# First half of the MLP as seven block products, with the high weight part streaming against both activation parts

## The chip, the cores and the metric

The kernel runs on one core of one Trainium2 chip. Its time is device microseconds (us) of one execution; of the kernel before, three runs gave a median of 2058.57 us (2057.65 to 2058.89). One more execution was taken with the hardware profiler, and all views below are of that one.

## The reference: what is computed

One encoder block on 512 tokens of width 2048, all in float32. `P`, `D` and `DFF` in the kernel are 128, 2048 and 8192. The change lies in the last three lines and in what leads over to them.

```python
h = rmsnorm(x, norm_mix_pre)
proj = h @ w_in                                  # 2048 x 5120
mix = concat(pool_mixer(...), hgrn2_mixer(...)) @ w_out
x = x + rmsnorm(mix, norm_mix_post)
h = rmsnorm(x, norm_mlp_pre)
ff = square(relu(h @ w_mlp_in)) @ w_mlp_out      # 2048 x 8192, then 8192 x 2048
x = x + rmsnorm(ff, norm_mlp_post)
```

## The kernel before

Every large matrix product keeps float32 accuracy with single-pass `float32r` products: each operand is split into a high part (a rounding copy on ACT) and a low part (the difference, on DVE), and a product of two blocks becomes three: high x high, high x low, low x high. The product of the low parts is left out. A weight block is 512 x 512 elements, 1024 KB; it is loaded raw, split in two halves (`w_split_gen` L200, later `split_gen` L875: 128x1024 elements per instruction), and used.

The stages, in order of time:

- **Input projection** (`pj`), the two mixers beside it, and the **output projection** (`om`, four groups of `gemm_group`, L258). The results of `om` are normed, added to the residual stream and kept in `Y` (`residual_task`, L768).
- **First half of the MLP** (`mi`, L947 to L960): 16 groups of 512 columns of `w_mlp_in`. The activations `h2` (transposed by `feed_h` on TensorE at L384, then split by ACT and DVE at L385 and L386) stay in SBUF as four pairs. In a group, each of four weight blocks is stationary in 128x128 pieces, and all 512 tokens stream against each piece: `block` (L241) issues `wh,ah`, `wh,al`, `wl,ah`. That is 16 groups x 4 blocks x 4 column pieces x 4 row pieces x 3 = 3072 products with 512 moving columns. Four PSUM banks collect a group; `evac_in` (L834) does relu and the row scale on DVE (L837), the square on ACT (L838), and writes the result to DRAM (`h1_dram`, L839).
- **Second half of the MLP** (L979 to L1072): for each of 8 pieces of 1024 rows of `w_mlp_out`, a 2 x 2 block scheme with seven products instead of eight (`ORDER`, L851). A slot is one of the seven products on one half `q` of the columns: 112 slots of 24 products (`products`, L979) with 512 moving columns. Here the activations are stationary and the weights stream. Sums of weight blocks are made by DMAs that add into SBUF (L889, from POOL's queue); sums of activation blocks by DVE (L910), which are then split (L906, L907). `act_steps` (L912) lists these steps, and `pend` (L1039) says from which slot each may be issued.
- **The end**: `finish_rows` (L1017) norms the result, adds the residual stream read back from DRAM, and writes the output: rows of the first 256 tokens at slot `base + 9`, the rest after the last slot.

Each engine works off its own queue in the order in which the program lists the instructions. In a slot, the split of the next slot's weights comes first on ACT and DVE, then what else is due. ACT can overwrite the high part `mHI` of slot k + 1 only once slot k - 1 has ended, since there are two `mHI` and two `mLO` tiles.

Of the kernel before, what the change touches and what calls it, by code (L numbers as in the profile page):

```python
# [28 lines left out]
def hybrid_block(  # L29
# [34 lines left out]
    psg_pool = tc.tile_pool(name="psg", bufs=4, space=PSUM)  # L64
    psg = psg_pool.__enter__()
# [4 lines left out]
    h1_dram = dram.tile([DFF, T], F32, name="h1_dram")  # L70
# [154 lines left out]
    def new_pair(nm):  # L225
        h = pairs.tile([P, 4, 512], F32R, tag="ph", name=nm + "h")
        l = pairs.tile([P, 4, 512], F32R, tag="pl", name=nm + "l")
        return h, l
# [26 lines left out]
    def new_banks(name):  # L255
        return [psg.tile([P, 512], F32, tag="g", name=f"{name}_{j}") for j in range(4)]

    def gemm_group(name, acts, w_stationary, evac, feeder=None, merge=0):  # L258
# [47 lines left out]
        if merge:  # L306
            ws = []
            for _ in range(merge):
                if wnext["split"] <= unit_no[0]:
                    w_split(4)  # L310
                    w_dma()
                ws.append(take_unit())
            if banks is None:
                banks = new_banks(name)
            for j in range(4):
                for k in range(merge):
                    ui = n - merge + k
# [3 lines left out]
                    clock.tick()  # L321

# [11 lines left out]

    for c in range(NC):
        for u in range(4):
            wlist.append((w1, u * 512, c * 512))
# [400 lines left out]
    def late_pools():  # L738
        clock.drain()
        hg.__exit__(None, None, None)  # L740
        yp = ctx.enter_context(tc.tile_pool(name="yp", bufs=1))
        tp2 = ctx.enter_context(tc.tile_pool(name="tp2", bufs=2))
        late["tp2"] = tp2
        late["Yall"] = yp.tile([P, NT, D], F32, name="Y")
        late["Y"] = [late["Yall"][:, t, :] for t in range(NT)]
# [18 lines left out]
    h2 = []  # L764
# [3 lines left out]
    def residual_task(t):  # L768

        Y = late["Y"]  # L770
        if t == 0:
            h2.extend(new_pair(f"h2{u}") for u in range(4))
        rt = row_rstd(t)
        for u in range(4):
# [4 lines left out]
            if t == 3:  # L779
                yield 1  # L780
        nc.gpsimd.dma_start(x2_dram[t * P:(t + 1) * P, :], Y[t])
        if t < 3:
            yield 3
            row_square(t)

    def feed_h(u, kt):
        Y = late["Y"]
        c = u * 512 + kt * P
        feed(h2[u], kt, [Y[t][:, c:c + P] for t in range(NT)], vcol("mpre", u * 4 + kt))

# [6 lines left out]
    def norm2_task():  # L797
        row_square(3)
        yield 1
# [4 lines left out]
        yield from row_bcast(rbc, rstd2)  # L804

    def load_xr(t):
        xr = pairs.tile([P, D], F32, tag="ph" if t < 2 else "pl", name=f"xr{t}")
        nc.gpsimd.dma_start(xr, x2d[t * P:(t + 1) * P, :])
        late["xr", t] = xr
# [13 lines left out]
    for n in range(4):  # L823
        if n == 2:
            for t in range(NT):
                load_xr(t)
        gemm_group(f"om{n}", MixActs(), False, evac_mix(n), merge=2 if n == 3 else 0)
    clock.add(norm2_task(), 4)
    keep_warm(12)


    tp2, Yall = late["tp2"], late["Yall"]

    def evac_in(c):  # L834
        def f(j, bank):
            r = tp2.tile([P, 512], F32, tag="tmp", bufs=2, name="r")
            nc.vector.scalar_tensor_tensor(out=r, in0=bank, scalar=0.0, in1=rbc, op0=ALU.max, op1=ALU.mult)  # L837
            nc.scalar.activation(out=r, in_=r, func=AF.Square)  # L838
            nc.gpsimd.dma_start(h1_dram[c * 512 + j * P:c * 512 + (j + 1) * P, :], r)  # L839
        return f  # L840
# [9 lines left out]
    NP = NC // 2  # L850
    ORDER = (1, 2, 5, 3, 6, 7, 4)  # L851
    slots = [(p, i, q) for p in range(NP) for i in ORDER for q in range(2)]
    st = {"X": {}, "YZ": {}, "HI": {}, "LO": {}, "A": {}, "r": {}, "S": {}}

    def w2_block(p, a, b, q):
        r0, c0 = (2 * p + a - 1) * 512, (2 * q + b - 1) * 512
        return w2[r0:r0 + 512, c0:c0 + 512].rearrange("(kt p) c -> p kt c", p=P)

    def load_x(x):

        if x < 2 * NP:
            nc.sync.dma_start(st["X"][x % 3], w2_block(x // 2, 1, 1, x % 2))

    def load_yz(n):

        if n < 4 * NP:
            p, k = divmod(n, 4)
            nc.sync.dma_start(st["YZ"][n % 3], w2_block(p, 2, 1 + k // 2, k % 2))

    def raw_of(p, i, q):  # L870
        if i in (1, 5, 6, 4):
            return st["X"][(2 * p + q) % 3]
        return st["YZ"][(4 * p + q + (0 if i == 2 else 2)) % 3]

    def split_gen(k):  # L875
        if k >= len(slots):
            return
        p, i, q = slots[k]
        raw, hi, lo = raw_of(p, i, q), st["HI"][k % 2], st["LO"][k % 2]
# [8 lines left out]
        if more:  # L888
            nc.gpsimd.dma_start(raw, w2_block(p, *more, q), accum_op=ALU.add)  # L889
        elif i == 4:  # L890
            load_x(2 * p + q + 3)
        else:
            load_yz(4 * p + q + (0 if i == 2 else 2) + 3)

    def load_r(p):
        if p < NP:
            for h in range(2):
                c = 2 * p + h
                nc.sync.dma_start(st["r"][h], h1_dram[c * 512:(c + 1) * 512, :].rearrange("(j p) t -> p j t", p=P))

    def r_block(tp, kh):
        return st["r"][kh - 1][:, :, (tp - 1) * 256:tp * 256]

    def split_a(i, src):
        a = st["A"][i]
# [3 lines left out]
    def sum_s(dst, a, b, op):  # L909
        nc.vector.tensor_tensor(out=st["S"][dst], in0=a, in1=b, op=op)  # L910

    def act_steps(p):  # L912

        S = st["S"]
        return [
            (1, lambda: split_a(1, r_block(1, 1))),
            (2, lambda: split_a(2, r_block(1, 2))),
            (0, lambda: sum_s(0, r_block(2, 1), r_block(2, 2), ALU.subtract)),
            (5, lambda: split_a(5, S[0])),
            (0, lambda: sum_s(1, S[0], r_block(1, 1), ALU.subtract)),  # L920
            (0, lambda: sum_s(0, r_block(1, 2), S[1], ALU.add)),
            (3, lambda: split_a(3, S[0])),
            (6, lambda: split_a(6, S[1])),
            (0, lambda: sum_s(1, r_block(1, 1), r_block(2, 1), ALU.subtract)),
            (7, lambda: split_a(7, S[1])),
            (4, lambda: (split_a(4, r_block(2, 2)), load_r(p + 1))),
        ]

    def new_act(i, tag):
        st["A"][i] = pairs.tile([P, 2, 4, 256], F32R, tag=tag, name=f"a{i}")  # L930

    def y_block(tp, n):
        return Yall[:, 2 * tp - 2:2 * tp, n * 512:(n + 1) * 512]

    def begin_split():
        for k in ("HI", "LO"):
            st[k][0] = wspl.tile([P, 4, 512], F32R, tag=k.lower(), name=f"m{k}0")
        return split_gen(0)

    def begin_x(x):  # L940
        st["X"][x] = wraw.tile([P, 4, 512], F32, tag="raw", name=f"X{x}")
        load_x(x)

    behind["dma"] = [lambda: begin_x(0), lambda: begin_x(1)]
    behind["split"] = [begin_split]

    for c in range(NC):  # L947
        gemm_group(f"mi{c}", h2, True, evac_in(c), feeder=feed_h if c == 0 else None)
        if c == NC - 4:
            for h in range(2):  # L950
# [144 lines left out]
```

## Time and profile before

| | |
|---|---|
| median of three runs | 2058.57 us |
| the profiled execution, its own time | 2058.64 us |
| its span (first to last instruction) | 2056.9 us |
| PE (matrix products) busy | 2028.0 us, 99% of the span |
| PEld (loads of the stationary operand) busy | 1680.0 us, 82% |
| DVE busy | 1065.0 us, 52% |
| ACT busy | 698.8 us, 34% |
| first product of `mi` to first product of the second half | 713.97 to 1418.42 us |
| last product | starts at 2042.6 us |

How to read it: PE is TensorE with its products, PEld the loads of its stationary operand, DVE is VectorE, ACT ScalarE, POOL GpSimd, SP the engine that issues most DMAs. The ends of products are modelled: the record of a 128x512 product lasts 0.39 us, but the next one starts long before. The pace of TensorE is therefore read from starts of successive products, not from busy time. A group's row gives busy us, mean ns of one instruction, and the idle time before it with what ended it. In the timeline the columns are start, duration, engine, line, operation, out<-in, shapes and count.

### The profile page before, as it was taken

The numbers are of one execution on the slowest core, as the hardware profiler recorded it, in microseconds if no ns is written. First come the engines' busy times: TensorE is split into PE (matmuls) and PEld (weight loads), VectorE is DVE, ScalarE is ACT, GpSimd is POOL, SyncE is SP. The second block draws the span as 40 slices with busy tenths as digits, with TensorE's granted clock in tenths as the row PEclk, the third lists the DMA queues.
The fourth block names the chain that finished last, engine by engine and source line by source line (L and its number), as shares of the span: only waits on it lengthen the run. The fifth ranks groups of instructions, "written<-read, shape, count | busy, mean of one in ns | idle before, by whom it ended". The sixth has DMA issues, their size and how long they took to land. (4 is left out here: it accounts for less than half of the span.)

```text
span 2056.9 us, 22509 instructions
## 1 busy us (share of the span) xinstructions
PE 2028.0 (99%) x9354; PEld 1680.0 (82%) x9354; DVE 1065.0 (52%) x1170; ACT 698.8 (34%) x865; POOL 130.7 (6%) x197
## 2 busy tenths in 40 slices
PE   9999999999999999999999999999999999999995
PEld 7888888888888888888888888887888888888884
DVE  4547443754623452222322222334778778778877
ACT  5322232223222342222222222223554444444443
POOL 1000000000000000000000000000110110110110
PEclk9999999999999999999999999999999999999998
DMA  5322222222353343433343333546998998998994
GB/s 189 109 82 82 83 80 84 83 66 80 108 188 103 123 143 123 123 119 106 118 146 114 114 123 108 178 145 186 239 222 210 227 224 217 224 221 225 218 214 134
DMA packets 144933, 302.43 MB, mean 147 GB/s; under 512 B 5752, under 2 KB 8896, under 8 KB 143040
## 3 DMA queue, kind: packets, MB, share of 16 engines
q1 hardware_dynamic: 104432, 207.64, 30.9%
q0 software_dynamic: 40400, 93.36, 21.4%
q8 instruction: 73, 1.20, 0.2%
q14 instruction: 28, 0.23, 0.0%
HBM read 275.81 MB, written 25.17 MB: 146 GB/s over the span
## 5 line engine op out<-in xcount | busy, mean ns | idle before, releaser
L216 DVE TENSOR_TENSOR wl<-wr,wh 128x1024 fp32r<-128x1024 f32 (+1 forms) x246 | 289.3, 1197 | 431.7 <-ACT wh L215 431.5
L215 ACT CAST wh<-wr 128x1024 fp32r<-128x1024 f32 (+1 forms) x246 | 244.9, 1024 | 387.4 <-PE mi L252 241.6
L987 PE MATMUL al<-mHI,a 128*128 128x512 f32 x1024 | 318.9, 391 | 1.5 <-ACT mHI L882 1.5
L987 PE MATMUL ga<-mHI,a 128*128 128x512 f32 x768 | 238.9, 391 | 1.6 <-ACT mHI L882 1.6
L987 PEld LDWEIGHTS al<-mHI,a 128*128 128x128 f32 x1024 | 193.5, 189 | 42.3 <-ACT mHI L882 1.9
L987 PE MATMUL al<-mLO,a 128*128 128x512 f32 x512 | 200.5, 392 | 5.4 <-DVE mLO L883 5.4
L882 ACT CAST mHI<-X 128x1024 fp32r<-128x1024 f32 x128 | 133.8, 1053 | 145.5 <-PE ga L987 69.9
L987 PEld LDWEIGHTS ga<-mHI,a 128*128 128x128 f32 x768 | 145.0, 189 | 32.2 <-ACT mHI L882 2.0
L883 DVE TENSOR_TENSOR mLO<-X,mHI 128x1024 fp32r<-128x1024 f32 x128 | 150.8, 1219 | 13.6 <-ACT mHI L882 13.6
L987 PE MATMUL ga<-mLO,a 128*128 128x512 f32 x384 | 150.4, 392 | 0.8 <-DVE mLO L883 0.8
L882 ACT CAST mHI<-YZ 128x1024 fp32r<-128x1024 f32 x96 | 100.5, 1054 | 118.4 <-PE al L987 64.4
L837 DVE SCALAR_TENSOR_TENSOR r<-mi,rbc 128x512 f32<-128x512 f32 x64 | 44.0, 688 | 165.6 <-PE mi L252 165.6
L838 ACT ACTIVATE r<-r 128x512 f32<-128x512 f32 x64 | 40.5, 632 | 261.9 <-DVE r L837 230.8
L987 PEld LDWEIGHTS al<-mLO,a 128*128 128x128 f32 x512 | 96.8, 189 | 25.9 <-DVE mLO L883 5.7
L883 DVE TENSOR_TENSOR mLO<-YZ,mHI 128x1024 fp32r<-128x1024 f32 x96 | 113.0, 1219 | 4.3 <-ACT mHI L882 4.3
L252 PE MATMUL mi<-h20h,wh 128*128 128x512 f32 x256 | 100.0, 391 | 0.8 <-ACT wh L215 0.8
L252 PE MATMUL mi<-h21h,wh 128*128 128x512 f32 x256 | 100.3, 392 | 0.0
L252 PE MATMUL mi<-h22h,wh 128*128 128x512 f32 x256 | 100.0, 391 | 0.0
L252 PE MATMUL mi<-h20h,wl 128*128 128x512 f32 x256 | 99.8, 390 | 0.1
L252 PE MATMUL mi<-h23h,wh 128*128 128x512 f32 x256 | 99.7, 389 | 0.0
L252 PE MATMUL mi<-h20l,wh 128*128 128x512 f32 x256 | 99.7, 389 | 0.0
L252 PE MATMUL mi<-h22h,wl 128*128 128x512 f32 x256 | 99.7, 389 | 0.0
(292 smaller groups left out, 3785.8 us busy)
## 6 DMA issues: line engine op xcount, KB each, us to landing
wr<-in_w_mlp_in SPq DMA_DIRECT2D x64, 1024.0 KB, 5.7
X<-in_w_mlp_out POOLq DMA_DIRECT2D x48, 1024.0 KB, 10.1
wr<-in_w_in SPq DMA_DIRECT2D x39, 1024.0 KB, 5.1
YZ<-in_w_mlp_out SPq DMA_DIRECT2D x32, 1024.0 KB, 6.4
wr<-in_w_out SPq DMA_DIRECT2D x16, 1024.0 KB, 5.1
h_dram<-r POOLq DMA_DIRECT2D x64, 256.0 KB, 3.6
r<-h_dram SPq DMA_DIRECT2D x16, 1024.0 KB, 10.1
X<-in_w_mlp_out SPq DMA_DIRECT2D x16, 1024.0 KB, 5.1
```

The lines of the kernel that those rows point to most:

```text
L215: nc.scalar.copy(out=hi[:, ks, :], in_=raw[:, ks, :])
L216: nc.vector.tensor_tensor(out=lo[:, ks, :], in0=raw[:, ks, :], in1=hi[:, ks, :].bitcast(F32), op=ALU.subtract)
L252: nc.tensor.matmul(bank, l, r, start=first and kt == 0 and oi == 0, stop=last and kt == 3 and oi == 2)
L837: nc.vector.scalar_tensor_tensor(out=r, in0=bank, scalar=0.0, in1=rbc, op0=ALU.max, op1=ALU.mult)
L838: nc.scalar.activation(out=r, in_=r, func=AF.Square)
L882: nc.scalar.copy(out=hi[:, ks, :], in_=raw[:, ks, :])
L883: nc.vector.tensor_tensor(out=lo[:, ks, :], in0=raw[:, ks, :], in1=hi[:, ks, :].bitcast(F32), op=ALU.subtract)
L987: nc.tensor.matmul(bank[:, h, :], a[:, l, kt, ts], r[:, kt, :], start=i in (1, 2, 5) and kt == 0 and oi == 0, stop=kt == 3 and oi == 2, sk ...
```

## The change

The first half of the MLP is written as 112 slots too, with the same seven products as the second half; one list of 224 slots covers both. The tokens are split in two halves of 256, the 2048 input rows in two halves of 1024, and a pair of 512-column weight blocks forms a piece `g` (8 pieces). A slot is one product on 512 of the 1024 input rows (`q`), and stationary is the weight, as before. The moving operand now has 256 columns. Two forms are used:

- In piece 0, three products of 256 columns per 128x128 piece: high x high, high x low, low x high (L1019).
- In pieces 1 to 7, the high weight part meets both activation parts in one product of 512 moving columns (256 of the high part, 256 of the low), whose two results lie side by side in one PSUM bank (L1014); the low weight part then meets the high activation part with 256 columns, added to the first of the two (L1015). The two halves of the bank are added when the bank is emptied (`evac_in`).

The diff, cut to the parts that are spoken of:

```diff
-    for c in range(NC):
-        gemm_group(f"mi{c}", h2, True, evac_in(c), feeder=feed_h if c == 0 else None)
-        ...
+    slots = [(g, i, q) for g in range(2 * NP) for i in ORDER for q in range(2)]
+    def w_block(g, a, b, q):
+        if g < NP:
+            w, r0, c0 = w1, (2 * (a - 1) + q) * 512, (2 * g + b - 1) * 512
+        else:
+            w, r0, c0 = w2, (2 * (g - NP) + a - 1) * 512, (2 * q + b - 1) * 512
...
+    plan = {
+        0: ([feed_step(1, 1, "act"), spl(1, 1, 1, 1)], [feed_step(1, 2, "dve")]),
+        1: ([lambda: new_act(2), spl(2, 0, 1, 2)], [feed_step(1, 3, "act")]),
...
+    def products_in(k, hook):
+        g, i, q = slots[k]
+        main = PA if i in (1, 6, 7, 4) else PG
...
+            if g:
+                o = main[m // 2][:, m % 2].rearrange("p (a b) -> p a b", a=2)
+                nc.tensor.matmul(o, hi[:, kt, ms], r, start=st, stop=False, skip_group_check=True)
+                nc.tensor.matmul(o[:, 0], lo[:, kt, ms], r[:, 0], start=False, stop=sp, skip_group_check=True)
+            else:
+                o = main[0][:, m // 2, (m % 2) * 256:(m % 2) * 256 + 256]
+                for oi, (l, x) in enumerate(((hi, 0), (hi, 1), (lo, 0))):
+                    nc.tensor.matmul(o, l[:, kt, ms], r[:, x], start=st and oi == 0 and m % 2 == 0,
+                                     stop=sp and oi == 2, skip_group_check=True)
+            if n % 4 == 3:
+                hook(n // 4)
...
+    for k in range(n_in):
+        def hook(n):
+            if n == 0:
+                while ends and "rbc2" in late:
+                    ends.pop(0)()
+            if n == 1:
+                for f in amid:
+                    f()
+                evac_in(k, 0)
+        w_split_all(k + 1)
+        for f in before:
+            f()
+        products_in(k, hook)
+        evac_in(k, 1)
+        run_pend(k, 1)
...
-    keep_warm(12)
...
-        if k == base + 9:
-            finish_rows(1)
-    finish_rows(2)
+        if d == 9:
+            for t in range(2):
+                steps.extend(finish_steps(t))
+        for _ in range(2):
+            if steps and d < 13:
+                steps.pop(0)()
```

What goes with it. The activations of the first half are no longer split token row by token row: their transposes (`feed_in`, the same 64 in number) go to raw tiles in SBUF, DVE forms their block sums there (`to_sum`, L893), and each of the seven operands is split (`split_in`, L889 and L890, or L885 and L886 with a minus sign). `plan` spreads these steps over slots 0 to 10. `evac_in` takes results out per half slot: copies on ACT (L1052), additions and subtractions on DVE (L1049, L1067), and `finish_in` does relu, scale and square per 128x1024. Weight sums of the first half come by adding DMAs from POOL's queue too. The second half keeps its products and their order; it has two tiles for the second kind of raw weight block where it had three, its first activation steps (`run_pend`) are issued during the last slots of the first half, the last slot runs its two PSUM banks one after the other, and the finishing steps are spread over slots instead of standing in one block. The 12 calls that kept TensorE busy between `om` and `mi` (`keep_warm`) are gone.

Two places in the order of the instructions. First, PE in the middle of the first half: `mi` is a PSUM bank, `h20h` and `h20l` the high and low activations, `wh` and `wl` the parts of a weight block. Before:

```order
L252 MATMUL mi_1_5361<-h20h,wh_5304 128x512
L252 MATMUL mi_1_5361<-h20l,wh_5304 128x512
L252 MATMUL mi_1_5361<-h20h,wl_5305 128x512
L252 MATMUL mi_1_5361<-h20h,wh_5304 128x512
L252 MATMUL mi_1_5361<-h20l,wh_5304 128x512
L252 MATMUL mi_1_5361<-h20h,wl_5305 128x512
```

The same place in the change; `mo` is a PSUM bank, `a` the activations with both parts, `mh` and `ml` the parts of a weight block:

```order
L1014 MATMUL mo_5629<-a_5098,mh_4643 128x512
L1015 MATMUL mo_5629<-a_5098,ml_4644 128x256
L1014 MATMUL mo_5629<-a_5098,mh_4643 128x512
L1015 MATMUL mo_5629<-a_5098,ml_4644 128x256
L1014 MATMUL mo_5630<-a_5098,mh_4643 128x512
L1015 MATMUL mo_5630<-a_5098,ml_4644 128x256
```

Where three products of 512 columns served 512 tokens, a product of 512 and one of 256 serve 256 tokens.

Second, DVE at the start of the first half. Before, between the residual of the last token rows (L777) and the steady groups, DVE splits weights (`wl`) and transposed activations (`h20l`, `h21l`):

```order
L386 SCALAR_TENSOR_TENSOR h20l<-fps,vec,h20h 128x512
L216 TENSOR_TENSOR wl_4724<-wr_4473,wh_4723 128x512
L777 SCALAR_TENSOR_TENSOR Y<-Y,rt,xr_4141 128x512
L386 SCALAR_TENSOR_TENSOR h20l<-fps,vec,h20h 128x512
L216 TENSOR_TENSOR wl_4724<-wr_4473,wh_4723 128x512
L777 SCALAR_TENSOR_TENSOR Y<-Y,rt,xr_4141 128x512
L386 SCALAR_TENSOR_TENSOR h21l<-fps,vec,h21h 128x512
L386 SCALAR_TENSOR_TENSOR h20l<-fps,vec,h20h 128x512
L216 TENSOR_TENSOR wl_4724<-wr_4473,wh_4723 128x512
```

In the change, in slots 4 and 5: `RU`, `YX` and `A` are raw activations and their sums, `a` the split operands, `ml` the low parts of the weights of slots 5 and 6:

```order
L858 TENSOR_TENSOR ml_4683<-X_4470,mh_4682 128x1024 x2
L893 TENSOR_TENSOR RU<-RU,A_4971 128x1024
L890 TENSOR_TENSOR a_4931<-RU,a_4931 128x1024
L890 TENSOR_TENSOR a_5029<-A_4886,a_5029 128x1024
L893 TENSOR_TENSOR A_4886<-A_4886,YX 128x1024
L893 TENSOR_TENSOR RU<-RU,A_4886 128x1024
L858 TENSOR_TENSOR ml_4644<-YZ_4680,mh_4643 128x1024 x2
L886 SCALAR_TENSOR_TENSOR a_5095<-A_4886,a_5095 128x1024
L890 TENSOR_TENSOR a_5098<-RU,a_5098 128x1024
```

The splits of weights now stand between sums and splits of activations of twice the size, and the operand of slot 5 (`a_4931`) comes after the sum that it is split from.

More of the change, by code (lines that the diff above doesn't have):

```diff
@@ L804, in norm2_task, with load_xr @@
         yield from row_bcast(rbc, rstd2)
[L806 to L809, printed above, removed]
+        late["rbc2"] = True
+    def load_xr(i):
+        xr = pairs.tile([P, 2, D], F32, tag="pp", name=f"xr{i}")
+        for k in range(2):
+            t = 2 * i + k
+            nc.gpsimd.dma_start(xr[:, k], x2d[t * P:(t + 1) * P, :])
+            late["xr", t] = xr[:, k]
     def evac_mix(n):
@@ new lines, in hybrid_block @@
+    behind["dma"] = [lambda: begin_x(0), lambda: begin_x(1)]
+    for n in range(4):
+        if n == 2:
+            load_xr(0)
+            load_xr(1)
+        last = n == 3
+        gemm_group(f"om{n}", MixActs(), False, evac_mix(n), merge=2 if last else 0,
+                   during=during_mix if last else None)
+    tp2, yp = late["tp2"], late["yp"]
+    YZ[0] = tp2.tile([P, 4, 512], F32, tag="big", bufs=1, name="YZ0")
+    load_yz(0)
+    HI[1] = wspl.tile([P, 4, 512], F32R, tag="hi", name="mh1")
@@ L929, in new_act @@
[L929 to L944, printed above, removed]
@@ new lines, in hybrid_block, with run_pend @@
+    pend = []
+    for p in range(NP):
+        for n, (i, free, f) in enumerate(act_steps(p)):
+            pend.append((p, i, f, n_in + 14 * p + max(free - 14, -8 + n)))
+    ready = set()
+    def run_pend(k, most=2):
+        for _ in range(most):
+            if pend and pend[0][3] <= k:
+                p, i, f, _at = pend.pop(0)
+                f()
+                if i:
+                    ready.add((p, i))
+    for k in range(n_in):
+        g = slots[k][0]
+        before, amid = plan.get(k, ([], []))
+        def hook(n):
[8 more added lines that the diff above has]
+        for f in before:
+            f()
+        products_in(k, hook)
+        evac_in(k, 1)
+        run_pend(k, 1)
+        clock.tick()
+        if k >= last_in:
+            begin_out(k - last_in)
+        if k == 13:
+            assert "rbc2" in late
+            pss_pool.__exit__(None, None, None)
+            psm = ctx.enter_context(tc.tile_pool(name="psm", bufs=1, space=PSUM, reuse_waits="tile"))
+            ps_mo = [psm.tile([P, 2, 512], F32, name=f"mo{q}") for q in range(2)]
+            PA, PG = ps_in[::-1], ps_mo
@@ L1001, in evac_out @@
             nc.scalar.copy(out=yv, in_=bank)
-        else:
-            nc.vector.tensor_tensor(out=yv, in0=yv, in1=bank, op=ALU.add if sign > 0 else ALU.subtract)
-        if p == NP - 1 and i in LAST:
-            n = 2 * q + b - 1
-            for t in (2 * tp - 2, 2 * tp - 1):
+            return
+        final = g == 2 * NP - 1 and i in LAST
+        end = k == len(slots) - 1
+        parts = [slice(h, h + 1) for h in range(2)] if end else [slice(0, 2)]
+        for hs in parts:
+            nc.vector.tensor_tensor(out=yv[:, hs], in0=yv[:, hs], in1=bank[:, hs],
+                                    op=ALU.add if sign > 0 else ALU.subtract)
+            if not final:
+                continue
+            for h in range(hs.start, hs.stop):
+                t = 2 * tp - 2 + h
```

464 lines of the change are left out of this document (291 added, 173 removed).

## The prediction

> **What bounds the kernel now.** I read the page's first part, then the table of stretches (us from the span's start: busy time of PE, PEld, DVE, ACT and POOL with their records, granted clock, DMA share, GB/s).
>
> ```profile
> PE 2028.0 (99%) x9354; PEld 1680.0 (82%) x9354; DVE 1065.0 (52%) x1170; ACT 698.8 (34%) x865; POOL 130.7 (6%) x197
> 760.00:1400.00 640.00, 640.00 (x2825) 530.14 (x2824) 183.31 (x181) 154.98 (x180) 31.83 (x59) 1.00 0.41 127
> 1420.00:2040.00 620.00, 610.65 (x2670) 503.79 (x2669) 489.81 (x433) 300.62 (x313) 80.76 (x64) 0.99 0.91 216
> ```
>
> TensorE bounds both halves of the MLP. In the first half everything else is idle most of the time (DVE 183 of 640 us, DMA 41%); in the second, with seven block products, DVE has 490 of 620 us and the DMA engines 91%, and TensorE still lost only some 9 us. So the first half is worth what its products cost, and the price of one is read from their starts. First and last of a run in the timeline of PE, 25 products apart, and one merged piece of the chain that ended last:
>
> ```profile
> 1000.00 0.39 PE L252 MATMUL mi<-h21h,wl 128*128 128x512 f32 x1
> ...
> 1005.67 0.39 PE L252 MATMUL mi<-h22h,wh 128*128 128x512 f32 x1
> 1466.66 43.52 PE al L987 x192
> ```
>
> 5.67 / 25 and 43.52 / 192 both give 0.2267 us for a product of 512 columns with its load. The first half's 3072 products are 696.4 us. Where the stage begins:
>
> ```profile
> 708.57 0.40 PE L252 MATMUL om<-wh,mp1l 128*128 128x512 f32 x1
> 708.80 2.84 PE L365 MATMUL warm_ps<-ones,ident 128*128 128x128 f32 x24
> 711.48 0.49 PE L384 MATMUL fps<-ident,Y 128*128 128x128 f32 x3
> 712.36 0.77 PE L384 MATMUL fps<-ident,Y 128*128 128x128 f32 x5 [0.39 <-DVE Y L777]
> 713.97 0.50 PE L252 MATMUL mi<-h20h,wh 128*128 128x512 f32 x1 [0.85 <-ACT wh L215]
> ...
> 1418.42 0.39 PE L987 MATMUL al<-mHI,a 128*128 128x512 f32 x1
> ```
>
> From 708.80 to 1418.42 are 709.6 us: 696.4 of products, 24 fillers in 2.68 us (0.112 each), 64 transposes at that pace 7.1, and 3.4 of waits and slow restarts.
>
> **The products.** The change has 8 pieces x 14 slots x 16 = 1792 pairs of a 128x128 weight piece and a row piece. In pieces 1 to 7 (1568 of them) each costs one product of 512 columns and one of 256; in piece 0 (224) three of 256. What 256 columns cost no row shows, so I bound it. Below stand, in the timeline, sixteen small products with a full 128x128 load each, the group of loads, and products at half clock with their stretch:
>
> ```profile
> 192.36 1.89 PE L603 MATMUL lps<-Q,K 128*128 128x64 f32 x16
> 194.06 0.48 PE L252 MATMUL pj<-wh,xT2h 128*128 128x512 f32 x1
> L987 PEld LDWEIGHTS al<-mHI,a 128*128 128x128 f32 x1024 | 193.5, 189 | 42.3 <-ACT mHI L882 1.9
> 1430.00:1435.00 5.00, 3.16 (x7) 2.33 (x8) 4.34 (x5) 4.78 (x6) 0.00 (x0) 0.74 0.71 131
> 1432.92 1.05 PE L987 MATMUL ga<-mHI,a 128*128 128x512 f32 x2
> 1433.78 0.63 PE L987 MATMUL ga<-mLO,a 128*128 128x512 f32 x1
> 1434.20 1.05 PE L987 MATMUL ga<-mHI,a 128*128 128x512 f32 x2
> 1435.06 0.63 PE L987 MATMUL ga<-mLO,a 128*128 128x512 f32 x1
> ```
>
> Small products with their loads start every 1.70 / 16 = 0.106 us, so a load can follow a load that fast, and the 189 ns of its record is latency. The fillers with 128 columns stand at 0.112. The floor for 256 columns is therefore 0.112. At half clock five products take 2.14 us, 0.428 each, so the array streams 512 columns in 0.214 at full clock, and 0.013 of the 0.2267 is something else. Is it a fixed part per product, 256 columns cost 0.107 + 0.013 = 0.120; does it scale, 0.113. I take 0.117: load and stream are nearly equal here, and neither can hide all of the other.
>
> The Trainium skill ("TensorE: Matmul & The Clock Gate", "Back-to-back issue gap") gives columns / 2.4 + 2.5 ns for a product by itself, 109 ns for 256 columns as an estimate, which would make the sum 18 us lower; for 512 columns it says 216 where this trace has 227, so I keep to the rows.
>
> Sum: 1568 x (0.2267 + 0.117) = 538.9, 224 x 3 x 0.117 = 78.6, together 617.5 us: **78.9 less** than 696.4. The 64 transposes stay; the 24 fillers go (**2.7 less**).
>
> **What must hide behind a slot.** A slot of pieces 1 to 7 lasts 16 x 0.3437 = 5.50 us. The durations:
>
> ```profile
> L882 ACT CAST mHI<-X 128x1024 fp32r<-128x1024 f32 x128 | 133.8, 1053 | 145.5 <-PE ga L987 69.9 <-PE al L987 66.9 <-ACT a L906 4.5
> L883 DVE TENSOR_TENSOR mLO<-X,mHI 128x1024 fp32r<-128x1024 f32 x128 | 150.8, 1219 | 13.6 <-ACT mHI L882 13.6
> L837 DVE SCALAR_TENSOR_TENSOR r<-mi,rbc 128x512 f32<-128x512 f32 x64 | 44.0, 688 | 165.6 <-PE mi L252 165.6
> L794 ACT ACTIVATE junk<-Y 128x512 f32<-128x512 f32 x16 | 9.8, 620 | 0.0
> 1976.38 2.36 DVE L883 TENSOR_TENSOR mLO<-X,mHI 128x1024 fp32r<-128x1024 f32 x2
> 1978.65 1.22 DVE L1003 TENSOR_TENSOR Y<-Y,ga 128x1024 f32<-128x1024 f32 x1
> ```
>
> Back to back, DVE starts a 128x1024 every (1978.65 - 1976.38) / 2 = 1.14 us. A piece needs of DVE 28 such halves of weight splits (31.9), 20 additions of 128x512 out of PSUM at 0.69 (13.8) and four final steps (4.6): 50 of 77 us. The tightest slot follows product 6: three additions (2.1), then two splits (2.3), which ACT's copies precede by 1.1: done some 5 us into 5.5. TensorE needs the second half only 0.7 us after its slot starts, so I cost this at nothing, with a slip of 1 us in each of 28 such places (28 us) as the price if the cover fails. Two products in a row on one bank (2 and 5, 6 and 7) leave half a slot, 2.7 us, to empty it; the additions need 1.4 to 2.1.
>
> DMA: 14 blocks of 1024 KB and 2 MB of results per piece, the same per slot as the second half, which ran so without a wait:
>
> ```profile
> 1590.00:1670.00 80.00, 80.00 (x354) 66.25 (x353) 64.41 (x56) 37.42 (x37) 10.20 (x8) 1.00 0.92 222
> X<-in_w_mlp_out POOLq DMA_DIRECT2D x48, 1024.0 KB, 10.1
> ```
>
> An adding DMA lands in 10.1 us and is needed four slots, 22 us, after it is issued. On POOL's queue the writes of `x2_dram` and `h1_dram` now stand among the adding DMAs; each waits for a DVE or ACT step no more than a slot away.
>
> **The start of the first half.** Here the cover is gone. Until slot 7 can begin, DVE must pass 34 instructions of 128x1024 (38.8), 16 of 128x512 (11.4) and 12 small ones (2.0): 52.2 us. It can begin 2.6 us after the last `om` product, because ACT's copy of the first weights stands behind four squares of 0.62 with a read of 0.19 each. Following both queues row by row I find some 8 us in which DVE waits for ACT. Slot 7 thus starts 62.5 us after `om`; TensorE's own work until then is 7 slots x 5.6 and 56 transposes, 45.6. That is 17 us of waits, in four pieces of 3 to 4 us (before slots 1, 5, 6, 7), plus 2.5 for a restart at half clock (above: after a wait at 1430 some 12 products at 0.428). **19 more**, bounded by 9 (no wait on ACT) and 28 (twice the waits); the 3.4 of before go.
>
> **Boundary and end.** The pieces of the chain around the second half:
>
> ```profile
> 1432.34 34.32 PE ga L987 x143
> ...
> 2017.56 0.16 DVE Y L1028
> 2017.71 1.04 issue
> 2018.75 3.93 DVE Y L1028 x5
> 2022.68 1.15 DVE mLO L883
> 2023.87 19.16 PE al L987 x71
> 2043.05 1.23 DVE Y L1003
> ...
> 2049.47 3.18 DVE Y L1028 x4
> ```
>
> From 1418.42 to 1466.66 the 192 products of eight slots need 43.5 us and took 48.2: 4.7 lost, as `h1_dram` had first to be read back and summed. In the change these steps are issued eight slots ahead: **4.2 less**. From 1466.66 to 2043.05 the other 2496 products need 565.9 and took 576.4: 10.5 lost, mainly to the finishing block at 2017. Spread over slots 9 to 12 it still puts about 7 us on a DVE that has 5.45, so I see three waits of 2 to 3.5 us: **1 less**. After the last product, 2043.05 to 2056.9, half of the last evacuation moves ahead of it: **1.5 less**.
>
> **Sum.** 2056.9 - 78.9 - 2.7 + 19 - 3.4 - 4.2 - 1 - 1.5 = 1984.2 of span; 1.7 lies outside it (2058.64 - 2056.9), and the profiled run equals the median within 0.1: **1986 us**.
>
> **Rivals.** *A, better:* 256 columns at the floor 0.112 (2240 x 0.005 = 11 less) and a start near its bound (10 to 13 less): 1962. For it speak the fillers at 0.112; against it the 0.013 that every long product shows. *B, slots slip:* evacuations and splits on DVE in one queue overrun, 1 us at 28 places: 2014. For it: 5 of 5.5 us in the tightest slot; against it: the second half ran at 64.4 of 80 us of DVE without a wait. *C, slower than before:* the load of the next weight piece does not hide behind a product of 256 columns, so that each costs load plus stream, 0.106 + 0.107 = 0.213. Then 2240 x (0.213 - 0.117) = 215 more: 2201. The point from which it decides is 0.149 per short product, where the 72 us of gain are used up. Against it: the fillers, whose loads and streams together take 0.112. The Trainium skill (same page, Part 3, "The mechanism") says that a load overlaps running products only when its row group differs, which would be this rival; the trace speaks against that, as 128-row loads do hide behind 512 columns at 0.2267. *That the change does not do what it says* is settled by the order: 512 and 256 alternate in pieces 1 to 7, and piece 0 alone has three short products.
>
> **Chances.** Forecast 0.68, A 0.12, B 0.13, C 0.07. The range holds A's 1962; above, 0.120 per product (7), the start's upper bound (9) and part of B (10) give 2012. A measurement here can tell 0.2%, 4 us. Faster: forecast, A and nearly all of B, 0.91; same 0.02; slower, C, 0.07.
>
> **What would show it.** Right: starts of successive `mo` products alternating 0.227 and about 0.117; slots of 5.5 us; waits on DVE (`a`, `ml`) in the first 62 us after `om`, none after slot 8; no wait at the boundary. Wrong: a pair of products above 0.36 us, waits of TensorE on DVE in every piece, or a DMA share at 1 with TensorE waiting for raw blocks.

## The result and the profile after

The changed kernel takes 2063.18 us (median of nine runs, 2059.75 to 2064.83) against 2057.96 us of the kernel before (nine runs beside it): ratio 1.0022, with an interval of 1.0011 to 1.0032. The forecast was 1986 us. The profiled execution took 2061.68 us, with a span of 2060.0. So 75.8 us of span had to be found between the forecast of 1984.2 and what came.

First the page's first part of the kernel after:

```profile
PE 1975.7 (96%) x10066; PEld 1665.3 (81%) x10066; DVE 1286.0 (62%) x1392; ACT 832.7 (40%) x1009; POOL 195.6 (9%) x229
```

TensorE is busy 52 us less than before, but 96% of the span where it was 99%. The work did shrink; waits have taken its place. Next the bounds of the stages, in the timeline of PE (start, duration, engine, line, operation):

```profile
743.79 0.39 PE L250 MATMUL om<-wh,mp 128*128 128x512 f32 x1
744.03 1.03 PE L913 MATMUL fps<-ident,Y 128*128 128x128 f32 x8
...
860.85 0.40 PE L1014 MATMUL mi<-a,mh 128*128 128x512 f32 x1
...
1000.08 0.40 PE L1014 MATMUL mi<-a,mh 128*128 128x512 f32 x1
1000.32 0.28 PE L1015 MATMUL mi<-a,ml 128*128 128x256 f32 x1
...
1005.63 0.40 PE L1014 MATMUL mi<-a,mh 128*128 128x512 f32 x1
...
1085.26 0.40 PE L1014 MATMUL mi<-a,mh 128*128 128x512 f32 x1
...
1087.38 0.40 PE L1014 MATMUL mi<-a,mh 128*128 128x512 f32 x1
...
1424.66 0.39 PE L1208 MATMUL mo<-mh,o 128*128 128x512 f32 x1
...
2045.05 0.39 PE L1208 MATMUL mo<-mh,o 128*128 128x512 f32 x1
```

The last product of `om` starts at 743.79; before, at 708.57. So 35.2 us were lost **ahead of** the first half, in stages whose products the change does not touch. The first half then takes 680.6 us (744.03 to 1424.66) where 709.6 stood before: 29 us won, not the 66 of the forecast. Sixteen pairs from 1000.08 to 1005.63 give 0.347 us a pair, six from 1085.26 to 1087.38 give 0.353; the forecast had 0.3437.

The list of waits of PE (line, who releases, us in total, times, longest) names the places. In the kernel before, the same list has no row of `om`, and of `pj` only two, at the start of the program:

```profile
PE mi L1014 <- DVE t L1049: 11.9, 7, 6.3
PE om L250 <- DVE Y L811: 11.7, 6, 4.0
PE mi L1019 <- ACT t L1052: 10.3, 6, 4.5
PE mi L1019 <- DVE t L1049: 7.1, 4, 4.6
...
PE pj L250 <- DVE pu L436: 3.8, 4, 1.5
PE pj L250 <- DVE F L515: 3.1, 4, 0.8
PE pj L250 <- ACT G L546: 3.1, 4, 0.8
PE pj L250 <- DVE Q L534: 2.2, 4, 0.8
PE om L250 <- DVE sst L753: 2.2, 2, 1.5
```

Everything that releases TensorE in these rows of `om`, of `pj` and of piece 0 (L1019) is an instruction that empties a PSUM bank, but for `sst` (L753), which DVE runs right behind such an emptying. One such place in the timeline of all engines:

```profile
691.97 0.39 PE L250 MATMUL om<-wh,mp 128*128 128x512 f32 x1
692.45 0.60 ACT L810 ACTIVATE junk<-om 128x512 f32<-128x512 f32 x1 [1.16 <-PE om L250]
...
693.17 0.69 DVE L811 TENSOR_TENSOR Y<-om,wpost 128x512 f32<-128x512 f32 x1 [0.61 <-ACT junk L810]
693.92 0.50 PE L250 MATMUL om<-wh,mp 128*128 128x512 f32 x1 [1.56 <-DVE Y L811]
...
694.26 0.40 PE L250 MATMUL om<-wl,mp 128*128 128x512 f32 x1
```

Bank after bank of a group is finished and emptied. TensorE, done with one bank at about 692.2, stands still until 693.92, when DVE has read that bank, though its next product writes another one. The wait costs more than its 1.56: from 691.97 to 694.26 two products take 2.29 us where two take 0.45 without a wait, 1.84 more. If each wait costs 0.28 more than its row has it, the 24 waits in the rows of `pj` and `om` (26.1 us) make up some 33 of the 35.2, an estimate. Two edits of the diff that the prediction did not speak of give the suspicion:

```diff
-    psg_pool = tc.tile_pool(name="psg", bufs=4, space=PSUM)
...
+    psg = ctx.enter_context(tc.tile_pool(name="psg", bufs=2, space=PSUM))
...
     def new_banks(name):
-        return [psg.tile([P, 512], F32, tag="g", name=f"{name}_{j}") for j in range(4)]
+        g = [psg.tile([P, 2, 512], F32, tag="g", name=f"{name}_{j}") for j in range(2)]
+        return [g[j // 2][:, j % 2] for j in range(4)]
```

The same four banks are held as two tiles of two banks. The suspicion is that a product that writes one bank of a tile then waits until the other bank of the same tile has been emptied.

### The profile page after: what moved, and what is told of

It is laid out like the page before. It is cut to its first block, busy times and chain, and to the rows that moved or that the text cites. A ratio compares the mean times of both kernels' runs of the same rounds, so it can differ in the third digit from the quotient of the medians.

```text
span 2060.0 us, 24502 instructions
## 1 busy us (share of the span) xinstructions
PE 1975.7 (96%) x10066; PEld 1665.3 (81%) x10066; DVE 1286.0 (62%) x1392; ACT 832.7 (40%) x1009; POOL 195.6 (9%) x229
## 4 chain that ended last, share of the span: by engine, by line
PE 88%; DVE 5%; ACT 2%; issue 1%; DMA 0%; DVEq 0%; ACTq 0%; POOLq 0%
PE pj L250 20%; PE mo L1208 16%; PE mi L1208 13%; PE mi L1014 9%; PE om L250 8%; PE mo L1014 8%; PE mi L1015 5%; PE mo L1015 4%; PE mi L1019 3%; PE lps L600 2%; DVE ml L858 1%; DVE t L1049 1%; ACT mh L857 0%; DVE YT L1258 0%; PE po L663 0%
## 5 line engine op out<-in xcount | busy, mean ns | idle before, releaser
L1014 PE MATMUL mi<-a,mh 128*128 128x512 f32 x896 | 316.5, 398 | 11.9 <-DVE t L1049 11.9
L1208 PE MATMUL mo<-mh,o 128*128 128x512 f32 x1024 | 318.5, 391 | 1.1 <-ACT mh L857 1.1
L250 PE MATMUL pj<-xT,wh 128*128 128x512 f32 x768 | 243.3, 397 | 10.9 <-DVE pu L436 3.8
L858 DVE TENSOR_TENSOR ml<-X,mh 128x1024 fp32r<-128x1024 f32 x176 | 207.4, 1220 | 70.3 <-ACT mh L857 70.3
L1015 PE MATMUL mi<-a,ml 128*128 128x256 f32 x896 | 251.1, 280 | 0.0
L1208 PE MATMUL mi<-mh,o 128*128 128x512 f32 x768 | 237.7, 389 | 0.0
L858 DVE TENSOR_TENSOR ml<-YX,mh 128x1024 fp32r<-128x1024 f32 x176 | 207.4, 1220 | 46.1 <-ACT mh L857 46.1
L1014 PE MATMUL mo<-a,mh 128*128 128x512 f32 x672 | 235.2, 395 | 0.0
L1208 PEld LDWEIGHTS mo<-mh,o 128*128 128x128 f32 x1024 | 192.9, 188 | 42.2 <-ACT mh L857 2.2
L1014 PEld LDWEIGHTS mi<-a,mh 128*128 128x128 f32 x896 | 169.3, 189 | 53.7 <-ACT mh L857 7.3
L1208 PE MATMUL mo<-ml,o 128*128 128x512 f32 x512 | 200.3, 391 | 6.4 <-DVE ml L858 6.4
L1015 PE MATMUL mo<-a,ml 128*128 128x256 f32 x672 | 187.5, 279 | 0.0
L1015 PEld LDWEIGHTS mi<-a,ml 128*128 128x128 f32 x896 | 170.0, 190 | 0.0
L1014 PEld LDWEIGHTS mo<-a,mh 128*128 128x128 f32 x672 | 126.1, 188 | 30.0
```

The lines of the kernel that those rows point to most:

```text
L250: nc.tensor.matmul(bank, l, r, start=first and kt == 0 and oi == 0, stop=last and kt == 3 and oi == 2)
L858: nc.vector.tensor_tensor(out=lo[:, ks, :], in0=raw[:, ks, :], in1=hi[:, ks, :].bitcast(F32), op=ALU.subtract)
L1014: nc.tensor.matmul(o, hi[:, kt, ms], r, start=st, stop=False, skip_group_check=True)
L1015: nc.tensor.matmul(o[:, 0], lo[:, kt, ms], r[:, 0], start=False, stop=sp, skip_group_check=True)
L1208: nc.tensor.matmul(bank[:, h, :], a[:, l, kt, ts], r[:, kt, :], start=i in (1, 2, 5) and kt == 0 and oi == 0, stop=kt == 3 and oi == 2, sk ...
```

## Experiments

Times are medians; each kernel ran beside the kernel before on the same chip (2057.2 to 2057.4 us), and the ratio's interval is given. Differences between kernels of different rounds are uncertain by about 1 us, since the medians of the kernel before differ by 0.8 (2057.2 to 2058.0). No kernel below leaves out any part of the computation.

### The tiles of two banks, put into the kernel before

```diff
-    psg_pool = tc.tile_pool(name="psg", bufs=4, space=PSUM)
+    psg_pool = tc.tile_pool(name="psg", bufs=2, space=PSUM)
...
-        return [psg.tile([P, 512], F32, tag="g", name=f"{name}_{j}") for j in range(4)]
+        g = [psg.tile([P, 2, 512], F32, tag="g", name=f"{name}_{j}") for j in range(2)]
+        return [g[j // 2][:, j % 2] for j in range(4)]
```

> The kernel before, with one edit: its four one-bank PSUM tiles of a group become two tiles of two banks, as in the change. Nothing else of the change. Theory A (a product that writes one bank of a tile waits until the other bank of the same tile has been emptied): the projections lose what the change lost there, the first mi product comes some 35 us later than 714, and the 16 groups of the first half lose 1.66 us each as the 10 groups of the input projection did in the change, 27 in all; time about 2119. Theory B (the loss comes from the operand pairs, whose high and low parts now lie in one SBUF tile, so that DVE's writes of the low part hold up TensorE's reads of the high part): no loss here, about 2058.

Measured: 2137.78 us, ratio 1.0389 [1.0368, 1.0410]. Its list of waits:

```profile
PE mi L252 <- DVE r L838: 37.0, 32, 1.5
PE om L252 <- DVE Y L819: 11.4, 6, 3.7
...
PE pj L252 <- DVE pu L440: 3.8, 4, 1.5
PE pj L252 <- DVE F L519: 3.1, 4, 0.8
PE pj L252 <- ACT G L550: 3.1, 4, 0.8
PE om L252 <- DVE sst L757: 3.1, 2, 1.6
PE pj L252 <- DVE Q L538: 2.2, 4, 0.8
```

With nothing else changed, the rows of `pj` and `om` come out as in the kernel after, to the tenth for `pj`, and the old first half gets two such waits in each of its 16 groups. The cause of those waits is the tile, not the block products. Their price was under-estimated, 2119 against 2137.8: the last `om` product starts 36.8 us later, as expected, but the first half lost 47.0 us where 27 were expected, its 32 waits being 37.0 of them.

### One-bank tiles in the changed kernel

```diff
-        g = [psg.tile([P, 2, 512], F32, tag="g", name=f"{name}_{j}") for j in range(2)]
-        return [g[j // 2][:, j % 2] for j in range(4)]
+        return [psg.tile([P, 512], F32, tag="g", name=f"{name}_{j}") for j in range(4)]
...
-    ps_in = [psg.tile([P, 2, 512], F32, tag="g", name=f"mi{k}") for k in range(2)]
-    PA, PG = ps_in[0:1], ps_in[1:2]
+    ps_in = [psg.tile([P, 512], F32, tag="g", name=f"mi{k}") for k in range(4)]
+    PA, PG = ps_in[0:2], ps_in[2:4]
```

(From slot 14 on it takes new tiles of two banks, as in pieces 1 to 7 one emptying instruction reads 256 columns of each of two neighbouring banks.)

> The change, with one-bank PSUM tiles again in the projections and in piece 0 of the first half; the two-bank tiles are opened after slot 13. Operand pairs stay in one tile. Theory A: the projections are back to their time before (last om product near 709 instead of 744), and piece 0 loses its false waits, some 10 to 13 of its 117 us, so that about 104 to 107 stay; together 45 to 48 less, about 2016. Theory B: the last om product stays near 744, time 2050 to 2063.

Measured: 2010.68 us, ratio 0.9774 [0.9759, 0.9789]. Its list of waits no longer has a row of `om` on an emptying step, and what is left in the first half is this:

```profile
PE mj L1014 <- DVE t L1049: 11.6, 7, 6.4
...
PE mi L1019 <- DVE a L890: 2.9, 3, 1.8
PE mi L1019 <- ACT t L1052: 1.8, 1, 1.8
PE mi L1019 <- DVE t L1049: 1.8, 1, 1.8
```

52.5 us came back, a little more than the 45 to 48 expected. The new names in the code (`mj` is the tile from slot 14 on) change nothing in the products.

### One-bank tiles in the projections alone

The edit above for `new_banks`; piece 0 keeps its two tiles of two banks, from a pool of its own:

```diff
+    psg_pool.__exit__(None, None, None)
+    psi_pool = tc.tile_pool(name="psi", bufs=1, space=PSUM, reuse_waits="tile")
+    psi = psi_pool.__enter__()
+    ps_in = [psi.tile([P, 2, 512], F32, name=f"mi{k}") for k in range(2)]
     PA, PG = ps_in[0:1], ps_in[1:2]
```

> The changed kernel with one-bank accumulator tiles in the projections alone; piece 0 of the first half keeps its two tiles of two banks. Theory A (the false waits in the projections and those in piece 0 are separate costs): the projections' last product returns to about 709 us from the span's start, 35 us less, piece 0 stays at 117 us against 100 with one-bank tiles: about 2063 - 35 = 2028 us, and the further 17 us to 2011 belong to piece 0. Theory B (piece 0 is slow because the projections end late or in a bad state, not by its own tiles): piece 0 falls to 100 us by itself and the time to about 2011 us.

Measured: 2031.12 us, ratio 0.9871 [0.9857, 0.9884]. The instructions on the tiles `om`, `mi` and `mj` (count, duration, first to last start), and the rows of its waits that stay:

```profile
L251 PE MATMUL om<-wh,mp x256: 388/389/394, 540.5 to 709.8; 128*128 128x512 f32 x128
```

```profile
L1022 PE MATMUL mi<-a,mh x448: 278/283/682, 714.7 to 830.0; 128*128 128x256 f32 x150
...
  ACT t L1055: 10.3, 6
  DVE t L1052: 7.1, 4
  DVE Y L811: 3.7, 1
```

The last `om` product is back at 709.8, and piece 0 has the very waits of the kernel after, 10.3 and 7.1. So the two costs are separate: by the medians 32.1 us in the projections (2063.18 - 2031.12), and 20.4 in piece 0 (2031.12 - 2010.68). The split is rough, since the third row, a wait of 3.7 us at the start of piece 0, came with the new pool. From the last `om` product to the first of piece 1 the traces have 117.1 us in the kernel after, 120.5 here and 101.7 with one-bank tiles throughout, so piece 0's own share is nearer 15.

### The first sums in another room

In pieces 1 to 7 of the kernel after, one wait of 6.32 us stands alone:

```profile
1406.08 1.23 DVE L1132 TENSOR_TENSOR S<-S,r 128x1024 f32<-128x1024 f32 x1 [5.32 <-DMA h_dram<-t]
1407.23 2.35 DVE L858 TENSOR_TENSOR ml<-YX,mh 128x1024 fp32r<-128x1024 f32 x2
...
1411.04 0.77 PE L1014 MATMUL mi<-a,mh 128*128 128x512 f32 x1 [6.32 <-DVE t L1049]
...
1416.30 0.43 PE L1014 MATMUL mi<-a,mh 128*128 128x512 f32 x1
```

Read it from the product at 1411.04 upwards: TensorE waits for an addition on DVE that empties its bank; that addition stands behind a weight split, and the split behind a sum for the **second** half (`S`), which waited 5.32 us. Its tile is one of three that the results of the first half use too (`tmp`), and the earlier content was still on its way to `h1_dram`. The edit gives the sums of the first piece a place in the output accumulators, which are idle then:

```diff
-        if dst not in SO:
-            SO[dst] = tp2.tile([P, 4, 256], F32, tag="tmp", bufs=3, name=f"S{dst}")
+        if len(pend) > 11 * (NP - 1) and dst not in SO0:
+            SO0[dst] = SO[dst] = M["y1" if dst == 0 else "y2"][:, 0, 0:1024].rearrange("p (a b) -> p a b", a=4)
+        elif len(pend) <= 11 * (NP - 1) and dst not in SO1:
+            SO1[dst] = SO[dst] = tp2.tile([P, 4, 256], F32, tag="tmp", bufs=3, name=f"S{dst}")
```

> The change, with another room for the two block sums of the second half's first piece: they lie in the output accumulators, which are not yet written then, instead of in the ring of three tiles from which the results of the first half are written to DRAM. Theory A (DVE stands in line behind a sum that waits for such a write to land, and TensorE behind DVE): the 6.3 us wait of TensorE at 1411 and the one at 1431 go, with their restarts at half clock: 8 to 11 less, about 2053. Rival (the write is late because the DMA engines are full, and the next slots' raw weight blocks would be late as well): the wait moves to a weight split, 0 to 3 less.

Measured: 2056.83 us, ratio 0.9995 [0.9986, 1.0005], 6.4 less than the kernel after. The one row of its waits that answers:

```profile
PE mi L1014 <- DVE t L1049: 7.3, 7, 2.0
```

The seven waits sum to 7.3 where they were 11.9, and the longest is now 2.0 where it was 6.3: that wait is now 2.0 where the other six are 0.8 to 1.0, and has not gone altogether, as the expectation of 8 to 11 us less would have had it. The cause, the shared ring, is shown; its price is 6.4.

### Both, twice

> Both edits of the two runs above in one kernel. If they act in different stretches, their gains add: 45 to 48 and 8 to 11 less, about 2006, faster than the kernel before by some 50 us. If the second gain was only cover for something later, about 2016 as with the first edit alone.

> The kernel with one-bank tiles and the first sums in the output accumulators once more, beside its kin on the same chip. If the two gains add, 2010.7 - 6.4 = 2004 to 2006 us; if only the wait moved, 2009 to 2011 us.

Measured: 2009.48 us, ratio 0.9772 [0.9757, 0.9787], and the second time 2007.14 us, ratio 0.9758 [0.9745, 0.9772]. Against the one-bank tiles alone (2010.68) that is 1.2 and 3.5 us less, where 6.4 were to come if the gains added. In the traces pieces 1 to 7 take 565.6 us with the tiles alone (810.78 to 1376.4) and 558.7 and 558.8 with both, so the gain in this stretch is there, as it is with the tiles of two banks (563.8 to 557.0). With the one-bank tiles some 1.5 us of it are not the edit's but due to the pace of the pairs, which is spoken of below. The medians can't show it: the eight runs of this kernel lie between 2005.6 and 2015.5 us, and its two profiled runs differ by 3.4 us with the same time in pieces 1 to 7. Their difference lies ahead of piece 1, which starts at 813.3 in one and at 809.8 in the other.

### The finish of a result, two slots later

What is left in each of pieces 1 to 7 is one wait of 0.8 to 2.0 us, where product 4 begins to write the accumulator that product 7 has just finished. VectorE of the kernel with both edits, at one of these places, in the timeline:

```profile
953.73 2.36 DVE L858 TENSOR_TENSOR ml<-X,mh 128x1024 fp32r<-128x1024 f32 x2 [2.06 <-ACT mh L857]
956.00 2.73 DVE L1049 TENSOR_TENSOR t<-t,mj 128x512 f32<-128x512 f32 x4
```

All four additions run in one go behind the weight split, although two of them could have been made half a slot earlier. The split is late since ScalarE's copy stands behind the square of product 6's result. The edit takes that finish out of the slots of product 7:

```diff
-                while ends and "rbc2" in late:
+                while ends and "rbc2" in late and slots[k][1] != 7:
```

> The kernel with one-bank tiles and the first sums in the output accumulators, with one edit: the finish of the sixth block product's tile (ReLU, scale and square) no longer stands in VectorE's and ScalarE's rows ahead of the weight split for the fourth product, but two slots later. Theory A (the 1.0 to 2.0 us that TensorE waits once in each of pieces 1 to 7 for the sums of the seventh product, before the fourth may write the same accumulator, come from that split, which the finish delays, and which stands ahead of the sums in VectorE's row): most of the 7.3 us go, about 2004 us. Theory B (they are the sums' own length, four additions of 0.69 us, behind the last product): no change, 2009 us. Theory C (the finish meets another slot's work and delays it): over 2011 us.

Measured: 2002.64 us, ratio 0.9736 [0.9722, 0.9749]; 4.5 less than its neighbour at 2007.14. VectorE at the same place:

```profile
954.22 2.36 DVE L858 TENSOR_TENSOR ml<-X,mh 128x1024 fp32r<-128x1024 f32 x2 [0.80 <-ACT mh L857]
956.72 1.41 DVE L1049 TENSOR_TENSOR t<-t,mj 128x512 f32<-128x512 f32 x2
959.49 1.41 DVE L1049 TENSOR_TENSOR t<-t,mj 128x512 f32<-128x512 f32 x2 [1.36 <-PE mj L1015]
```

The additions come in two pairs, the first in the middle of the slot, and the row of `mj` waiting for additions of `t` is gone from its list of waits (7.6 us in seven before). Theory A holds for the waits. The time is a poorer witness: pieces 1 to 7 became 12.1 us shorter in the trace (558.8 to 546.7), more than the waits, since fewer pairs fell on the dearer of the two paces spoken of below; and 5.1 us were lost elsewhere, in piece 0 (101.7 to 104.3 from the last `om` product) and in the first eight slots of the second half (45.5 to 48.0).

### What the 512-column product is worth

```diff
-                nc.tensor.matmul(o, hi[:, kt, ms], r, start=st, stop=False, skip_group_check=True)
+                nc.tensor.matmul(o[:, 0], hi[:, kt, ms], r[:, 0], start=st, stop=False, skip_group_check=True)
+                nc.tensor.matmul(o[:, 1], hi[:, kt, ms], r[:, 1], start=False, stop=False, skip_group_check=True)
```

> The kernel with one-bank tiles and the first sums in the output accumulators, but in pieces 1 to 7 the product of the high weight part with both activation parts (512 columns) is made as two of 256 columns; piece 0 is made so already. Theory A (the 512-column product saves what the rows say): three products of 256 columns take 0.36 us in piece 0 (its pure pace), a pair 0.345, so 1568 x 0.015 = 24 us more, about 2033 us. Theory B (the price of 256 columns rises when weight loads come every 0.117 us without a longer product between them, as in the rival with the dear 256-column product: load not hidden): 0.213 apiece, 1568 x (0.64 - 0.345) = 460 us more, about 2470 us. Theory C (the longer product gains nothing, since it is two passes anyway): 2009 us. All of the same work, no part of the computation is left out.

Measured: 2021.21 us, ratio 0.9822 [0.9808, 0.9835], 14.1 more than its neighbour without the edit. Products in its timeline, 24 steps apart:

```profile
899.91 0.28 PE L1014 MATMUL mj<-a,mh 128*128 128x256 f32 x1
900.03 0.28 PE L1015 MATMUL mj<-a,mh 128*128 128x256 f32 x1
...
902.79 0.28 PE L1014 MATMUL mj<-a,mh 128*128 128x256 f32 x1
```

2.88 / 24 = 0.120 us for a product of 256 columns with its own load: the upper of the prediction's two bounds, and no trace of the dear load of rival C (0.213). Three of them are 0.360. Theory A was right in kind, but 24 us were expected and 14 came: the pairs of the neighbour were dearer than 0.345 (0.349 on average), and the longer slot also hid 2.5 us of the waits above (5.1 in place of 7.6).

### The pace of a pair

Away from waits, averages over 22 to 66 pairs in all these traces of alternating pairs show only two values, 0.3467 and 0.3533 us. The value changes at a wait of TensorE; where the later finish has taken the waits away, it changed at the first product of a piece, after a lag of up to 0.14 us that the list of waits does not have. The split kernel has 0.360 throughout. Two orders were tried on the kernel with the later finish: the low product ahead of the high one, and two of each in turn.

> The kernel with one-bank tiles, the first sums in the output accumulators and the later finish; in pieces 1 to 7 the product with the low weight part (256 columns) is made ahead of the one with the high part (512) instead of behind it. The question is the pace of a pair, which has two values in all runs so far, 0.3467 and 0.3533 us, and changes between them only at a wait. Theory A (the pace depends on how the alternation of the two lengths was entered): the same two values, in some other mixture; 2000 to 2011 us. Theory B (the order within the pair sets it): one value throughout, 0.3467 (about 2001) or 0.3533 (about 2011).

> The same base, but in pieces 1 to 7 two products of 512 columns follow each other and then two of 256. Theory A (the alternation of lengths is what locks to one of two paces): a pair's share becomes 0.2267 + 0.120 = 0.3467, the paces of each kind standing alone (512 columns in the second half, 256 in the run with the split product), throughout: about 2001 us. Theory B (the second pace has nothing to do with the alternation): both values remain, 2000 to 2011 us. Theory C (two changes of length for two pairs cost less than two for one): below 0.3467, about 1996 us.

Measured: 1999.58 us, ratio 0.9723 [0.9707, 0.9739], and 1997.27 us, ratio 0.9708 [0.9694, 0.9723]. With the low product first both paces are still there, 0.3467 up to 1043 us and 0.3533 after it; rows of its timeline, two pairs apart in each stretch (0.69 and 0.71 us):

```profile
1019.85 0.39 PE L1015 MATMUL mj<-a,mh 128*128 128x512 f32 x1
...
1020.54 0.39 PE L1015 MATMUL mj<-a,mh 128*128 128x512 f32 x1
...
1080.05 0.40 PE L1015 MATMUL mo<-a,mh 128*128 128x512 f32 x1
...
1080.76 0.40 PE L1015 MATMUL mo<-a,mh 128*128 128x512 f32 x1
```

With two and two there is one pace, 0.348 us a pair, in every stretch of 66 pairs in pieces 1 to 7: the alternation of single products is what has two paces. 0.3467 as the sum of the lone prices (0.2267 + 0.120) was expected; 0.348 came. Which of the two an alternating stretch falls into, and by what mechanism, stays open.

What the last kernel gains over its base (2002.64) was not measured side by side, and the traces show no gain in the changed stretch: pieces 1 to 7 take 546.7 us in the base, 550.6 with the low product first and 547.6 with two and two. Against the kernel before it is the fastest version here: 60 us, 2.9%.

## Why the prediction was wrong

In the order of time, from the kernel before's trace, the forecast and the trace after:

| term | forecast, us | measured, us | miss |
|---|---|---|---|
| `pj` and `om`, to the last `om` product (708.57 before, 743.79 after) | 0 | +35.2 | 35.2 |
| transposes, piece 0 and its start (744.03 to 860.85) | 104.7 | 116.8 | 12.1 |
| pieces 1 to 7 (860.85 to 1424.66) | 538.9 | 563.8 | 24.9 |
| second half (1424.66 to 2045.05; 624.2 before) | 619.0 | 620.4 | 1.4 |
| after the last product starts (14.3 before) | 12.8 | 15.0 | 2.2 |

**The step that failed** is the one that is not in the text: no term for the PSUM tiles, so that stages outside the first half were carried over at no change, and the start of piece 0 was worked out from DVE's and ACT's queues alone. What an edit changes in *the tile that a wait is attached to* was not gone through. Shown by three runs: added to the kernel before it costs 80 us, taken out of the changed one it gives back 52.5, and taken out of the projections alone 32.1. The Trainium skill (PSUM — Partial Sum Buffer, "PSUM bank collisions raise a hardware error") asks to guard PSUM "by **bank × quadrant** (by bank is the simple version), not by address"; here the guard was coarser than a bank, and the 37.0 us in 32 waits of the first experiment are what this cost, in a place where a guard by bank had none. The Trainium skill's page Perfetto Trace Analysis ("Matmuls") advises that independent groups rotate through PSUM banks, so that the emptying of one overlaps the next; the trace agrees only as far as banks are also separate tiles, since the changed kernel rotates through the same four banks as before.

**The products.** The mechanism was right: 512 and 256 alternate, and the short product's load hides. The price was a little low. In the trace after, 640 of the 1568 pairs run at 0.3533 and the rest at 0.3467, mean 0.3494 against 0.3437: 9 us of the 24.9. The short product alone costs 0.120, not 0.117. The estimate by the Trainium skill's formula for a product by itself (TensorE: Matmul & The Clock Gate, "Back-to-back issue gap", 109 ns) is further off than the bounds from the rows.

**"I cost this at nothing"** (DVE in steady slots) failed by 11.9 us, of two kinds: one wait of 6.3 us, told under the boundary, and a wait in each of the other six pieces, 5.6 us together (11.9 - 6.3), a weaker form of rival B: six places of 0.9 us and not 28 of 1 us. The text had named waits of TensorE on DVE in every piece as a sign against itself, and they came. The prediction gave "half a slot" to empty an accumulator that is written twice in a row; it named the pairs 2 and 5, 6 and 7, and missed 7 and 4, and it did not see that a late weight split lets the first half of the emptying slip too. The later finish showed both: the waits went.

**Boundary, "4.2 less".** The steps of the second half issued eight slots ahead made the boundary shorter, its first eight slots taking 45.5 us where 48.1 stood before (43.5 would be without waits), so 2.6 less and not 4.2; two waits of 0.57 and 0.76 us at 1430.9 and 1432.1 stayed, where none was forecast. And one of these steps brought a wait of 6.3 us to slot 110, by a tile ring that both halves share. After that wait TensorE ran at half clock; a stretch of the table with the granted clock (third figure from the right):

```profile
1411.00:1414.00 3.00, 2.96 (x9) 2.60 (x10) 2.96 (x4) 0.00 (x0) 0.00 (x0) 0.50 0.94 333
```

The next eight pairs (1411.04 to 1416.30 in the fence on that wait) took 5.3 us, 2.5 more than at 0.3467. 9 + 11.9 + 2.5 are 23.4 of the 24.9; the rest, 1.5, I put down to the slow first products behind the other six waits.

**The start, "19 more".** With the false waits gone, `om`'s end to piece 1 takes 101.5 us (709.27 to 810.78 in the run with one-bank tiles) against the 104.7 forecast. The sum is near, its terms are less so: of waits there are 9.9 us (6.5 in the three rows of `mi` above, 3.4 in four shorter ones) where 17 were expected; 5.6 of them are for split operands and weights, the mechanism of the forecast, and 4.3 for the emptying of a bank, which it did not have. In the changed kernel itself the waits for operands are down to 2.8, since TensorE came late by waiting for banks. Those waits are longer, and after the longest (4.6, 4.5 and 2.1 us) its trace has a granted clock of 0.5, from 778.1 to 784.9, 798.6 to 805.4 and 829.3 to 832.7 us; with one-bank tiles there is one such stretch in piece 0, of 3.4 us.

**The end, "1.5 less".** It became 0.7 longer than before, as nothing moved ahead of the last product:

```profile
2045.47 0.69 DVE L1233 TENSOR_TENSOR YT<-YT,mo 128x512 f32<-128x512 f32 x1 [0.65 <-PE mo L1208]
```

DVE empties the first bank of the last slot here. It starts 0.42 us after the start of the last product, which released it, though the last twelve products write the other bank only. Both banks are one tile, so this looks like the same cause, which no run separates here. It explains 0.65 us at most, as DVE was busy with the slot before until 2044.8; the rest of the 2.2 stays open.

**Rivals and range.** Rival C is refuted (0.120, not 0.213). Rival A's floor of 0.112 did not come. Without the two shared rooms the kernel takes 2007.1 and 2009.5 us: a gain of 48 to 50 where 72 were forecast, inside the range, but near its upper end of 2012, and most of what is missing lies in pieces 1 to 7 (558.8 against 538.9). The chance of 0.07 for slower lay wholly on a mechanism that did not occur, and 0.02 was left for a time that hardly changes, which is what came.

## What to carry over

Before pricing the work, list for every on-chip tile that the diff reshapes which instructions wait for which through it: a tile over two banks, or a ring shared by two stages, makes a wait where the data has no dependence, and it does so in stages that the change never meant to touch. A TensorE that is busy for 99% of the span had no slack here, so such waits of 1 to 2 us came in full and with a slow restart on top (47.0 us in the old first half for 37.0 of waits); the reshaped tiles alone cost 52.5 us, more than all the rest of the change had won (2058.0 - 2010.7 = 47.3). A wait that shows up on TensorE is to be followed back through the queue of the engine that releases it: here twice the late instruction was not the one named, and once it was not even of the same stage.

## What the hardware showed unexpectedly

- Alternating products of 512 and 256 columns run at one of two paces, 0.3467 or 0.3533 us a pair, and keep it for tens of microseconds at a granted clock of 1.00; it changes at waits or at the start of a piece. Over a piece of 224 pairs that is 1.5 us, over pieces 1 to 7 up to 10. Whether it makes the runs of one kernel scatter is not shown: two traces of one kernel had it in about the same number of pairs. In groups of two and two there is one pace, 0.348.
- A product of 256 columns with a load of its own takes 0.120 us when only such products follow each other, which is more than 256/512 of the 0.2267 of a long one (0.113). The two lengths fit a part of some 0.013 per product, the rest going with the columns (an estimate from these two rows); it does not reach down to 128 columns, where the fillers of the kernel before took 0.112 and not 0.067.
